# Second layer's value products: the high and the low part of the gated values side by side in one product of 448 columns

## The chip, the cores and the metric

One core of a Trainium2 chip. The metric is the device time of one execution in microseconds (us). The core's engines, by the names of the profile: PE (TensorE, products), PEld (its weight loads), DVE (VectorE), ACT (ScalarE), POOL (GpSimd) and SP (SyncE, which here issues most loads). Products write to accumulators in PSUM, whose banks hold 512 columns of 4 bytes for each of 128 partitions.

## The reference, cut to what matters

The model has two layers of mixers and a feed-forward part with 128 x 128 experts, of which each token takes 16 in each of 8 heads. The part around the change:

```python
eidx = jnp.take_along_axis(cand_i, fpos, axis=-1)
gate = jax.nn.softmax(fs, axis=-1)
act = jax.nn.gelu(jnp.einsum('td,thkd->thk', xb, u[eidx]).astype(F32), approximate=False)
w = (gate * act).astype(xb.dtype)
return jnp.einsum('thk,thkd->td', w, v[eidx])
```

The result f is added to the stream as x + g2 * f. Layer 0 has 512 tokens (256 of context, 256 latent), layer 1 only the 256 latent ones. At the end stands one more norm.

## The kernel before, in words

The kernel computes this densely for most tokens: every expert's activation for every token (u_blocks), times a gate that is zero for experts not chosen, times every expert's value row (v_blocks). 128 tokens of layer 0 and 32 of layer 1 are done apart by gathering their rows (tokens_apart, lines 1379 to 1435); so the dense products have wd = 384 columns in layer 0 and 224 in layer 1 (line 122).

Products at full precision are made of three products of a faster format. A number is split into a high part (a cast on ScalarE) and a low part (a subtraction on VectorE), and mm3 (lines 70 to 74) adds high x high, high x low and low x high:

```python
mm(ps, ah, bh, start=first, stop=False, **kw)
mm(ps, ah, bl, start=False, stop=False, **kw)
mm(ps, al, bh, start=False, stop=last, **kw)
```

The value stage of a layer (peer, lines 1179 to 1200) goes over 64 pairs of blocks; a block is 128 experts. For each pair, v_blocks

- loads 1 MB of values (line 1488) into one of two raw buffers;
- takes the pair's activations: for 20 of the pairs of layer 1 they have stayed in the tile "kept", already gated; otherwise they are loaded (va, line 1496), and the gates too, once for two pairs (vg, line 1493), and multiplied on VectorE (line 1500);
- splits the gated values into wh (ScalarE, line 1501) and wl (VectorE, line 1502), one instruction for both blocks, in a pool with two buffers in layer 0 and three in layer 1 (VA, line 33);
- splits each block's values into vh (line 1505) and vl (line 1506), in a pool of 10 buffers; a raw buffer is loaded again once both are done;
- issues the products: for each block and each of 8 output blocks d of 128 features, the three products of mm3 with vh or vl as weights and wh or wl as the moving operand, into the accumulator f of that d, columns 32 to 256 in layer 1. Each accumulator is one PSUM bank.

The loads go through SP's queue in the order in which they are issued. The engines' orders are made by the framework's planner from an estimate of durations, but for the last pair: there the order of TensorE, VectorE and ScalarE is that of the code (line 1530 on). In it the first block's products lead by three, each d gets its last products, the rows that were gathered for the tokens apart are added (line 1537), and then VectorE adds the accumulator, times g2, to the stream xt (line 1543). ScalarE squares xt (ss_add, line 338), VectorE adds squares in twos (line 340), and TensorE sums them over the partitions (line 346). In layer 1 the final norm and the output follow (final, lines 1554 to 1568).

Of the kernel before, what the change touches and what calls it, by code (L numbers as in the profile page):

```python
# [9 lines left out]
F32R = mybir.dt.float32r  # L10
# [4 lines left out]
ALU = mybir.AluOpType  # L15
# [38 lines left out]
class Kernel:  # L54
# [1425 lines left out]

    def v_blocks(self, l, n, i, acc, ts, off):

        w = self.wd[l]
        q = slice(off, off + w)
        parts = []
        nc, vp = self.nc, self.vp
        v = self.raw.tile([128, 2048], F32, name="raw").rearrange("p (b d) -> p b d", b=2)
        nc.sync.dma_start(v, self.A["v"][l, i:i + 2].rearrange("b p d -> p b d"))
        fold = i < 2 * FOLD[l]
        a = self.kept[:, i:i + 2] if fold else vp.tile([128, 2, w], F32, name="va")  # L1490
        if i % 4 == 0 and not fold:
            self.vg = vp.tile([128, w // 32, 4, 32], F32, name="vg", bufs=2)
            nc.sync.dma_start(self.vg[:, :w // 32].rearrange("p q b t -> p q (b t)"),
                              self.gd[l][:, :, i:i + 4].rearrange("q p b t -> p q (b t)"))
        if not fold:
            nc.sync.dma_start(a[:, :, :w], self.ad[l][i:i + 2].rearrange("b p t -> p b t"))
        wh, wl = (vp.tile([128, 2, w], F32R, name=x) for x in ("wh", "wl"))
        if not fold:
            av = a[:, :, :w].rearrange("p b (q t) -> p b q t", t=32)
            nc.vector.tensor_mul(av, av, self.vg[:, :w // 32, i % 4:i % 4 + 2].rearrange("p q b t -> p b q t"))  # L1500
        nc.scalar.copy(wh, a[:, :, :w])  # L1501
        nc.vector.tensor_tensor(wl, a[:, :, :w], wh.bitcast(F32), op=ALU.subtract)  # L1502
        for b in range(2):
            vh, vl = (self.spl.tile([128, 1024], F32R, name="spl") for _ in range(2))
            nc.scalar.copy(vh, v[:, b])  # L1505
            nc.vector.tensor_tensor(vl, v[:, b], vh.bitcast(F32), op=ALU.subtract)  # L1506
            parts.append((vh, vl, wh[:, b], wl[:, b]))

        def mm(d, b):
            c = slice(d * 128, (d + 1) * 128)  # L1510
            vh, vl, wh, wl = parts[b]
            self.mm3(acc[d][:, q], vh[:, c], vl[:, c], wh, wl, n + b == 0, n + b == 64)
        if n < 63:
            for b in range(2):
                for d in range(KD):
                    mm(d, b)
            return
        if l == 0:
            self.wraw, self.wspl = self.raw, self.spl
            self.nextg = self.gsplit(self.gload(self.A["win"][1, 9]))  # L1520
            self.nextq = self.wdma(self.A["win"][1, 2])
        full = ts.stop - ts.start
        if l == 0:
            big = [vp.tile([128, 2, 1024], F32, name="csb", bufs=1).rearrange("p a b -> p (a b)")]
            big += [vp.tile([128, 1024], F32, name="adaw", bufs=1), self.row_tile()]
            sqs = [t[:, a:a + 512] for t in big for a in range(0, t.shape[-1], 512)]
        else:
            sqs = [vp.tile([128, full], F32, name="sq", bufs=KD) for _ in range(KD)]
        self.ss_begin(sqs)
        with self.order("PE", "DVE", "Activation"):  # L1530
            lead = 3
            for d in range(lead):
                mm(d, 0)
            for d in range(KD):
                mm(d, 1)
                if off:
                    nc.tensor.matmul(acc[d][:, 0:off], self.facc[:, d * 128:(d + 1) * 128], self.fsel, start=True, stop=True)  # L1537
                if d + lead < KD:
                    mm(d + lead, 0)
                for s, seg in ((1, CTX), (0, LAT)):  # L1540
                    if seg.start >= ts.start:
                        o = slice(seg.start - ts.start, seg.stop - ts.start)
                        nc.vector.scalar_tensor_tensor(self.xt[:, d, seg], acc[d][:, o], self.mod[l][:, 5, d, s:s + 1],  # L1543
                                                       self.xt[:, d, seg], op0=ALU.mult, op1=ALU.add)
                if d == 1:
                    ps = self.pf.tile([128, 512], F32, name="f0")
                self.ss_add(d, self.xt[:, d, ts])
                if d > 2 and d % 2:
                    self.ss_mm((d - 3) // 2, ps)
            self.ss_mm(3, ps)  # L1550
            self.ss_mm(4, ps)
            self.ss_end(ps, full, 1024, self.ms, sqs[1])
# [250 lines left out]
```

## Time and profile before

| what | us |
|---|---|
| median of 3 runs (2806.03, 2815.85, 3308.41) | 2815.85 |
| the profiled execution | 2815.21 |
| its span | 2813.4 |
| second layer's value products, from about | 2431 |
| to about | 2800 |

In the rows, L73 is line 73 of the kernel; "f<-wl,spl" says that the instruction writes the tile f and reads wl and spl (vh and vl are both called spl, the raw values raw). Shapes are partitions x elements. "x1024" is a number of instructions. A duration in the profile is that of one instruction from its start to its modelled end; products overlap, so their pace is read from the distance of their starts, or from their number in a stretch without gaps. Arrows in a view of waits name who was waited for.

### The profile page before, as it was taken

The page shows a single profiled execution, that of the slowest core. Times are in us where ns is not written, and L with a number is a line of the kernel's source. Part 1 is how long each engine was busy: PE and PEld are TensorE (multiplying, and loading weights), DVE is VectorE, ACT ScalarE, POOL GpSimd, SP SyncE. Part 2 cuts the span into 40 slices and gives each one's busy share as a digit, 9 for nine tenths or more (in the row PEclk, how much of TensorE's full clock was granted, in tenths as well). Part 3 has the DMA queues.
Part 4 walks back from the last instruction along what each step waited for, and adds up shares of the span by engine and source line. Part 5 has one row for each costly group of instructions (what it writes and reads, how often), then busy time and mean ns, then how long its engine had stood idle before and what let it go on. Part 6 is the DMA issues. An engine that isn't in the chain of part 4 may idle for free. (4 is left out here: it accounts for less than half of the span.)

```text
span 2813.4 us, 46689 instructions
## 1 busy us (share of the span) xinstructions
PE 2649.8 (94%) x18167; PEld 2446.7 (87%) x18167; DVE 2166.6 (77%) x4491; ACT 1244.3 (44%) x2059; POOL 478.8 (17%) x419
## 2 busy tenths in 40 slices
PE   8989899999999998899999998988999999899998
PEld 5766768999998898899999997767899999899998
DVE  5665657999998875799999887555888778577765
ACT  5564635334443443333333334644544445344443
POOL 0010000003333333234333310100001101211110
PEclk9999899999999999899999999999999999999999
DMA  7110424647999989899999993202545878888884
GB/s 266 65 61 31 165 90 161 225 148 262 351 371 332 339 325 377 306 361 382 384 374 376 376 322 115 77 33 72 203 145 188 299 266 306 319 310 304 292 292 161
DMA packets 275742, 691.62 MB, mean 246 GB/s; under 512 B 18016, under 2 KB 145376, under 8 KB 266048
## 3 DMA queue, kind: packets, MB, share of 16 engines
q1 hardware_dynamic: 196608, 448.12, 45.6%
q0 software_dynamic: 46080, 167.79, 15.8%
q10 hardware_dynamic: 32832, 72.72, 6.9%
q8 instruction: 142, 2.33, 0.3%
q14 instruction: 80, 0.66, 0.1%
HBM read 616.56 MB, written 71.57 MB: 245 GB/s over the span
## 5 line engine op out<-in xcount | busy, mean ns | idle before, releaser
L72 PE MATMUL pu<-h2h,spl 128*128 128x384 f32 (+1 forms) x2048 | 637.3, 311 | 40.7 <-ACT spl L1448 27.7
L73 PE MATMUL f<-wl,spl 128*128 128x384 f32 (+1 forms) x2048 | 623.9, 306 | 8.0 <-DVE wl L1502 8.0
L74 PE MATMUL pu<-h2h,spl 128*128 128x384 f32 (+1 forms) x2048 | 628.9, 308 | 2.6 <-DVE spl L1449 2.6
L73 PE MATMUL pu<-h2l,spl 128*128 128x384 f32 (+1 forms) x2048 | 629.5, 307 | 0.0
L74 PE MATMUL f<-wh,spl 128*128 128x384 f32 (+1 forms) x2048 | 609.7, 305 | 2.3 <-DVE spl L1506 2.3
L72 PE MATMUL f<-wh,spl 128*128 128x384 f32 (+1 forms) x2048 | 568.4, 307 | 8.8 <-ACT act L1466 4.6
L72 PEld LDWEIGHTS pu<-h2h,spl 128*128 128x128 f32 x2048 | 393.2, 192 | 49.6 <-ACT spl L1448 32.4
L73 PEld LDWEIGHTS f<-wl,spl 128*128 128x128 f32 x2048 | 391.5, 191 | 10.9 <-DVE wl L1502 10.4
L74 PEld LDWEIGHTS pu<-h2h,spl 128*128 128x128 f32 x2048 | 392.7, 192 | 4.4 <-DVE spl L1449 4.2
L72 PEld LDWEIGHTS f<-wh,spl 128*128 128x128 f32 x2048 | 386.0, 191 | 10.7 <-ACT act L1466 5.0
L73 PEld LDWEIGHTS pu<-h2l,spl 128*128 128x128 f32 x2048 | 393.3, 192 | 0.3
L1505 ACT CAST spl<-raw 128x1024 fp32r<-128x1024 f32 x256 | 264.9, 1050 | 289.5 <-DMA raw<-in_v 202.8
L74 PEld LDWEIGHTS f<-wh,spl 128*128 128x128 f32 x2048 | 385.8, 191 | 2.8 <-DVE spl L1506 2.8
L1506 DVE TENSOR_TENSOR spl<-raw,spl 128x1024 fp32r<-128x1024 f32 x256 | 308.4, 1219 | 93.4 <-ACT spl L1505 85.1
L1448 ACT CAST spl<-raw 128x1024 fp32r<-128x1024 f32 x256 | 265.7, 1048 | 240.3 <-DMA raw<-in_ut 94.8
L1449 DVE TENSOR_TENSOR spl<-raw,spl 128x1024 fp32r<-128x1024 f32 x256 | 310.3, 1218 | 47.9 <-ACT spl L1448 38.3
L1409 POOL DMA_INDIRECT spl<-in_un,ix x97 | 129.3, 1333 | 716.7 <-DVE fp L1263 241.6
L1466 ACT ACTIVATE act<-pu 128x384 f32<-128x384 f32 (+1 forms) x216 | 93.0, 435 | 303.8 <-PE pu L74 280.7
L427 DVE TENSOR_TENSOR spl<-raw,spl 128x512 fp32r<-128x512 f32 (+1 forms) x226 | 149.4, 699 | 65.4 <-ACT spl L423 56.3
L1409 POOL DMA_INDIRECT row<-in_vn,ix x87 | 125.4, 1441 | 374.6 <-DVE facc L1422 316.3
L1501 ACT CAST wh<-va 128x768 fp32r<-128x768 f32 (+1 forms) x108 | 78.3, 725 | 231.3 <-DVE va L1500 131.6
L72 PE MATMUL fp<-s,spl 128*128 128x512 f32 (+1 forms) x416 | 161.2, 387 | 2.1 <-DVE s L666 1.2
(319 smaller groups left out, 4459.0 us busy)
## 6 DMA issues: line engine op xcount, KB each, us to landing
raw<-in_ut SPq DMA_DIRECT2D x128, 1024.0 KB
raw<-in_v SPq DMA_DIRECT2D x128, 1024.0 KB
ad<-act ACTq DMA_DIRECT2D x64, 384.0 KB
gd<-gstage ACTq DMA_DIRECT2D x12, 2048.0 KB
vg<-gd SPq DMA_DIRECT2D x32, 768.0 KB
va<-ad SPq DMA_DIRECT2D x64, 384.0 KB
raw<-in_win SPq DMA_DIRECT2D x22, 1024.0 KB
raw<-in_wq SPq DMA_DIRECT2D x16, 1024.0 KB
```

What stands on the lines that cost most here:

```text
L72: mm(ps, ah, bh, start=first, stop=False, **kw)
L73: mm(ps, ah, bl, start=False, stop=False, **kw)
L74: mm(ps, al, bh, start=False, stop=last, **kw)
L427: return eng.tensor_tensor(p[1][o], w[:, o], p[0][o].bitcast(F32), op=ALU.subtract)
L1409: nc.gpsimd.indirect_dma_start(r, None, tabs[which], bass.IndirectOffsetOnAxis(ix[:, s:s + 1], 0))
L1448: self.pin(nc.scalar.copy(uh, self.u[:, n % 2]), n < 3)
L1449: self.pin(nc.vector.tensor_tensor(ul, self.u[:, n % 2], uh.bitcast(F32), op=ALU.subtract), n < 3)
L1466: nc.scalar.activation(a[:, b, :w], ps[:, :w], AF.Gelu)
L1501: nc.scalar.copy(wh, a[:, :, :w])
L1505: nc.scalar.copy(vh, v[:, b])
L1506: nc.vector.tensor_tensor(vl, v[:, b], vh.bitcast(F32), op=ALU.subtract)
```

## The change

In layer 1 (wide = l > 0) wh and wl lie side by side in one tile wt, and each vh is multiplied with both at once: 448 columns, into columns 32 to 480 of the accumulator. The first 224 of them hold high x high, and low x high is added there as before; the other 224 hold high x low. At the end VectorE adds both halves to xt, one after the other. In the last pair's second block low x high goes ahead of the wide product, which closes the accumulation. In layer 0 only the tile is another; its products are those of mm3.

```diff
-        wh, wl = (vp.tile([128, 2, w], F32R, name=x) for x in ("wh", "wl"))
+        wide = l > 0
+        wt = vp.tile([128, 2, 2, w], F32R, name="wt")
+        wh, wl = wt[:, :, 0], wt[:, :, 1]
...
-            parts.append((vh, vl, wh[:, b], wl[:, b]))
+            parts.append((vh, vl, wh[:, b], wl[:, b], wt[:, b].rearrange("p a t -> p (a t)")))
 
         def mm(d, b):
             c = slice(d * 128, (d + 1) * 128)
-            vh, vl, wh, wl = parts[b]
-            self.mm3(acc[d][:, q], vh[:, c], vl[:, c], wh, wl, n + b == 0, n + b == 64)
+            vh, vl, wh, wl, both = parts[b]
+            first, last = n + b == 0, n + b == 64
+            if wide:
+                if last:
+                    nc.tensor.matmul(acc[d][:, q], vl[:, c], wh, start=False, stop=False)
+                nc.tensor.matmul(acc[d][:, off:off + 2 * w], vh[:, c], both, start=first, stop=last)
+                if not last:
+                    nc.tensor.matmul(acc[d][:, q], vl[:, c], wh, start=False, stop=False)
+            else:
+                self.mm3(acc[d][:, q], vh[:, c], vl[:, c], wh, wl, first, last)
...
+                if wide:
+                    seg = slice(ts.start + off, ts.stop)
+                    nc.vector.scalar_tensor_tensor(self.xt[:, d, seg], acc[d][:, off + w:off + 2 * w], self.mod[l][:, 5, d, 0:1],
+                                                   self.xt[:, d, seg], op0=ALU.mult, op1=ALU.add)
```

## Rows read from the trace of the kernel before

**Rows 1.** The page: busy time, share of the span and instructions of each engine.
```profile
PE 2649.8 (94%) x18167; PEld 2446.7 (87%) x18167; DVE 2166.6 (77%) x4491; ACT 1244.3 (44%) x2059; POOL 478.8 (17%) x419
```

**Rows 2.** Busy PE, PEld, DVE, ACT, POOL by stretch; granted clock, DMA share, GB/s.
```profile
2420.00:2440.00 20.00, 15.36 (x107) 14.99 (x107) 8.29 (x10) 5.41 (x9) 3.71 (x3) 0.83 1.05 389
1500.00:1520.00 20.00, 20.00 (x117) 20.00 (x116) 18.55 (x23) 7.41 (x8) 9.11 (x6) 1.00 1.04 386
2460.00:2520.00 60.00, 60.00 (x540) 60.00 (x539) 42.36 (x50) 27.44 (x33) 7.75 (x7) 1.00 0.89 315
2460.00:2780.00 320.00, 309.31 (x2732) 306.17 (x2731) 227.72 (x260) 140.67 (x172) 33.48 (x32) 1.00 0.86 294
```

**Rows 3.** Groups by line and shape, 2430 to 2813: busy, mean ns, idle before.
```profile
L73 PE MATMUL f<-wl,spl 128*128 128x224 f32 x1024 | 280.8, 277 | 8.0 <-DVE wl L1502 8.0
L72 PE MATMUL f<-wh,spl 128*128 128x224 f32 x1024 | 280.0, 277 | 6.7 <-ACT act L1466 4.6 <-ACT spl L1505 2.1
...
L1506 DVE TENSOR_TENSOR spl<-raw,spl 128x1024 fp32r<-128x1024 f32 x126 | 152.0, 1220 | 46.9 <-ACT spl L1505 44.4 <-PE f L73 1.3 <-PE f L74 1.0
L1505 ACT CAST spl<-raw 128x1024 fp32r<-128x1024 f32 x126 | 130.0, 1048 | 173.6 <-DMA raw<-in_v 155.2 <-PE f L73 10.4 <-PE f L74 8.0
...
L1500 DVE TENSOR_TENSOR va<-va,vg 128x448 f32<-128x448 f32 x44 | 27.4, 625 | 54.0 <-DMA va<-ad 32.8 <-issue 18.5 <-DVE wl L1502 2.8
L1502 DVE TENSOR_TENSOR wl<-va,wh 128x448 fp32r<-128x448 f32 x44 | 27.2, 620 | 6.5 <-ACT wh L1501 6.5
...
L1543 DVE SCALAR_TENSOR_TENSOR xt<-f,mod,xt 128x256 f32<-128x256 f32 x8 | 3.8, 481 | 5.6 <-PE f L1537 5.6
```

**Rows 4.** Who waited for whom, 2430 to 2813: us in total, times, longest.
```profile
ACT spl L1505 <- DMA raw<-in_v: 155.2, 50, 6.9
...
ACT wh L1501 <- PE f L74: 26.1, 10, 4.8
...
PE f L73 <- DVE wl L1502: 8.0, 12, 1.2
```

**Rows 5.** ScalarE in order of time: start, us, instruction, and the wait before it.
```profile
2517.37 1.05 ACT L1505 CAST spl<-raw 128x1024 fp32r<-128x1024 f32 x1 [4.01 <-DMA raw<-in_v]
...
2571.49 2.00 ACT L1505 CAST spl<-raw 128x1024 fp32r<-128x1024 f32 x2 [3.55 <-DMA raw<-in_v]
...
2588.94 1.05 ACT L1505 CAST spl<-raw 128x1024 fp32r<-128x1024 f32 x1 [5.56 <-PE f L73]
...
2644.92 1.05 ACT L1505 CAST spl<-raw 128x1024 fp32r<-128x1024 f32 x1 [3.35 <-DMA raw<-in_v]
...
2655.65 1.05 ACT L1505 CAST spl<-raw 128x1024 fp32r<-128x1024 f32 x1 [0.19 <-PE f L74]
...
2663.63 1.05 ACT L1505 CAST spl<-raw 128x1024 fp32r<-128x1024 f32 x1 [5.51 <-DMA raw<-in_v]
...
2760.98 1.05 ACT L1505 CAST spl<-raw 128x1024 fp32r<-128x1024 f32 x1 [3.41 <-DMA raw<-in_v]
```

**Rows 6.** SyncE's queue in order of time: the issue of one value load.
```profile
2656.99 0.37 SPq L1488 DMA_DIRECT2D raw<-in_v  x1
```

**Rows 7.** TensorE in order of time: first and last of 13 products of 512 columns.
```profile
438.12 0.40 PE L73 MATMUL mm<-h2l,spl 128*128 128x512 f32 x1
...
440.86 0.39 PE L73 MATMUL mm<-h2l,spl 128*128 128x512 f32 x1
```

**Rows 8.** VectorE in order of time at the end of the value stage.
```profile
2793.99 0.48 DVE L1543 SCALAR_TENSOR_TENSOR xt<-f,mod,xt 128x256 f32<-128x256 f32 x1 [4.74 <-PE f L1537]
...
2796.20 0.96 DVE L1543 SCALAR_TENSOR_TENSOR xt<-f,mod,xt 128x256 f32<-128x256 f32 x2
2797.64 0.43 DVE L340 TENSOR_TENSOR sq<-sq 128x256 f32<-128x256 f32 x1 [0.48 <-ACT sq L338]
2798.00 0.48 DVE L1543 SCALAR_TENSOR_TENSOR xt<-f,mod,xt 128x256 f32<-128x256 f32 x1
...
2800.20 0.87 DVE L1543 SCALAR_TENSOR_TENSOR xt<-f,mod,xt 128x256 f32<-128x256 f32 x2
```

## The prediction

> **What bounds the kernel now.** I read the first lines of the page first: TensorE's products are busy 2649.8 of 2813.4 us [rows 1], so work taken off TensorE can count, if nothing else in that stage is just as slow. The share is an average over stages, so I then cut out the one stage that the change touches, the second layer's value products, from about 2431 to 2800 us. In the table of stretches [rows 2] the reader is to see three things: in 2460 to 2520 the products are busy without a gap and 540 of them start in 60 us; over the whole of 2460 to 2780 they are busy 309.3 of 320 us; and the transfers run at 0.86 to 0.89 of the DMA engines while this goes on. The groups by line [rows 3] give the counts: each of the three product lines (72 and 73 stand there) starts 1024 products of 224 columns in this stage, and the two splits of the values run 126 times each in that window. Their last part is the waiting time of the engine in front of the line: TensorE waits 8.0 + 2.1 us on operands and 4.6 us on the stage before, which is little. The view of who waited for whom gives the other half: ScalarE waits 155.2 us in 50 pieces for the 1 MB loads of values, against 26.1 us in 10 [rows 4] and 10.4 + 8.0 us [rows 3] for TensorE to give a buffer back.
>
> So two paces lie close together: that of the products, and that of the supply (load, cast, subtraction, next load into the same one of two buffers). I call two blocks that come with one load a pair; the stage has 64. The products of a pair are 48, at 60 us / 540 = 111 ns each: 5.33 us. The supply is read from the starts of each pair's first cast, in stretches that show ScalarE waiting for loads alone from behind their first cast on [rows 5]. From 2517.37 to 2571.49 lie 10 pairs, 5.41 us each; from 2588.94 to 2644.92 another 10, 5.60 each; from 2655.65 to 2760.98 lie 18, 5.85 each. There the supply is already the slower one, and TensorE gets through on the blocks it has in hand. In one of these stretches a load that is issued at 2656.99 [rows 6] is waited for until 2663.63 [rows 5], 6.6 us; a buffer then spends two casts of 1.05 us and two subtractions of 1.22 us [rows 3] before it is loaded again, and VectorE has the gate products and the gathered rows between them. Nothing in that ring is a product.
>
> **The products.** The change takes away 2 x 1024 products of 224 columns (lines 72 and 73) and adds 1024 of 448. No product of 448 columns stands in the trace, so its pace is bounded by neighbours at the full clock: 384 columns go at 20 us / 117 = 171 ns [rows 2], 512 columns at (440.86 - 438.12) / 12 = 228 ns [rows 7]. Half way between 384 and 512 lies 448: 200 ns, which I take. Two narrow products cost 222 ns, so one merge saves 22 ns, and the stage 1024 x 22.2 ns = 22.7 us of TensorE's time, or 0.355 us a pair; by the ends it would be 52 us saved or 6 us lost. The reason for a saving is in the same rows: 224 columns take 111 ns, and 384 take only 60 ns more for 160 columns, 0.375 ns a column, so some 27 ns of a product don't grow with its columns by these two, and one such part goes with each merge; by 384 and 512, whose slope is 0.445 ns, it is nearly nothing. That is why I go by the point between the two nearest and not by either line.
>
> One rule stands against a saving. The Trainium skill (TensorE: Matmul & The Clock Gate, section "Wait — 56ns, not 53.3ns?") says that back-to-back products start N / 2.4 GHz plus about 2.5 ns apart once the clock is up. The rows don't agree with it at 224 columns: 111 ns stand against 95.8 ns by the rule, and 228 against 215.8 at 512. By the rule a merge would save only its 2.5 ns, an estimate of 2.6 us for the stage, and with the longer end below the kernel would come out where it was.
>
> **What of it reaches the end.** In the 38 pairs of the three stretches the supply sets the pace, and faster products only wait longer: nothing gained. In the other 26 pairs TensorE has no gap or holds the buffers (the 26.1 + 10.4 + 8.0 = 44.5 us that ScalarE waits for it), and I count the full gain: 26 x 0.355 = 9.2 us. The lower end for this term is 0, if the supply takes over at once there too (with 4.98 us a pair it would need 5.33 / 4.98 x 315 = 337 GB/s in the stretch of [rows 2] that now moves 315; 389 and 386 GB/s stand in other rows there, so the transfers as such allow it). The upper end is all 22.7 us, if supply is slow only because TensorE gives buffers back late.
>
> **The end of the stage.** The value stage's end now has eight more operations on VectorE, each 128 x 224, which add the second half of the accumulator. The same operation on 256 columns takes 0.481 us [rows 3]; for 224 I take 0.45, bounds 0.42 and 0.48. They can't hide. Today the updates of the end run from 2793.99 to 2800.20 + 0.87 = 2801.07 [rows 8], with gaps in which VectorE waits for the products. In the middle, from 2796.20 to 2798.00, two blocks take VectorE 1.80 us: two updates of 0.48, then 0.48 of waiting for ScalarE's square, then an addition of 0.43. Two more updates make that 2.70. Three such rounds and a last one of 4 operations, 1.77, are 9.87 us against 7.08 now: +2.8 us, on the path; bounds 2.4 and 3.5. Each square now waits for the second update of its block, which is in the 2.70. Behind it the same norm, root and output follow. In the last block the order of the two products is turned round; their number is that of the others.
>
> **What I count at nothing.** The two halves of the gated values become one tile. Its buffers are as many (two in the first layer, three in the second), and the last reader of the pair is the same low-part product, so buffers come free when they did. The casts write two runs of 224 with a gap instead of 448 in one; the gate product, which reads the gates in such pieces, takes 0.625 us against 0.620 for the subtraction [rows 3], so a gap costs some 5 ns, 64 x 3 x 5 ns = 1 us of two engines with room. The wide product waits for the subtraction that makes the low half; today its second narrow product does, one product later: at most 0.11 us in each of 12 waits [rows 4], 1.3 us. Were VectorE's order such that this subtraction came after one more of 1.22 us in every pair, 64 x 1.22 = 78 us would be the end of it; the order is planned anew, and nothing shows it. In the first layer only the tile changes and no product; TensorE is busy 20.00 of 20 us there [rows 2].
>
> **Sum.** The profiled execution took 2815.2 us, 1.8 us of it around its span of 2813.4, and the median of the three runs is 2815.85, so the two are one number here. 2815.2 - 9.2 + 2.8 = 2808.8, say 2809 us.
>
> **Rivals.** First, products pace the whole stage: all 22.7 us arrive, 2815.2 - 22.7 + 2.8 = 2795. For it: TensorE is busy 309 of 320 us. Against it: the 155.2 us of waiting for loads, and intervals above 5.33 us in 38 pairs. Second, slower than before: the supply takes over in the other 26 pairs as well, from the point where a pair of supply takes 5.33 us, and the longer end is all that is left: 2815.2 + 2.8 = 2818, and 2825 if the wide product goes no better than 512 columns do (228 ns, 1024 x 6 ns). For it: the stretch from 2460 to 2520 already runs the transfers at 0.89. Against it: the 44.5 us in which ScalarE waits for TensorE show a supply that is ahead in those pairs. Beside it stands a drop of the granted clock when gaps grow: 2420 to 2440, where the stage before ends and TensorE was busy 15.36 of 20 us, had a mean of 0.83 and 107 products where 180 fit [rows 2]; such a thing all through would cost far more. Third, only the columns count and a merge is worth nothing: 448 columns at 2 x 111 ns, gain 0, and the end's 2.8, 2818 again, told from the second by the pace of the wide products; the line through 384 and 512 columns speaks for it, the one through 224 and 384 against it. By the Trainium skill's rule above, an estimate of 2.6 us would be gained here, and the sum be 2815.
>
> **How the numbers follow.** Forecast 0.5, centre 2809, by itself 2800 to 2814. Products pace everything: 0.2, around 2795. Supply paces everything: 0.17, 2818 to 2825. Only columns count: 0.08, 2818. An order of VectorE or of the loads that is planned worse: 0.05. Two of the three runs of before, 2806.03 and 2815.85, lie 10 us apart, so the range reaches to both first rivals and a little over: 2790 to 2823. Two per cent are 56 us, about what a measurement of this kernel can tell from no change. A gain over it would need the 384 columns' pace and a supply that follows: 0.01. A loss over it needs the bad order or the clock: 0.03. Within: 0.96.
>
> **What would show it.** Right, step by step: 1024 products of 128 x 448 and 1024 fewer products in all; wide products starting 200 ns, narrow ones 111 ns apart in a stretch without gaps; ScalarE's waits for the value loads longer than 155 us and its waits for TensorE shorter than 44.5; TensorE's own waits in the stage up from some 15 to some 28 us; 16 updates at the end and 2.8 us more from the first to the last. Wrong: wide products at 215 ns or more, a stage shorter by 20 us, waits of TensorE for the low half in most pairs, or a difference that lies in the first layer.

## The result, and the profile after

| | before | after |
|---|---|---|
| median of 6 runs each, us | 2813.07 | 2798.97 |
| the profiled execution, us | 2815.21 | 2801.05 |
| its span, us | 2813.4 | 2799.3 |

The ratio is 0.9942, with an interval of 0.9917 to 0.9967: some 16 us less (9 to 23). It leaves out before's run of 3308.41 us, which was in a slower state. The forecast was 6.4 us less. That lies below the interval; the stated range, 2790 to 2823 us, holds the result.

Where the 14.1 us between the two spans lie can be added up from starts in TensorE's and VectorE's order of time. I cut at the last activation product (writes pu), the first value product (writes f), the first update of xt and the end of the last update:

| stretch, us | before | after | difference |
|---|---|---|---|
| start to last activation product | 2427.54 | 2427.28 | -0.3 |
| to the first value product ("gap") | 4.3 | 1.7 | -2.6 |
| to the first update ("stage") | 362.1 | 347.6 | -14.5 |
| to the end of the last update | 7.1 | 9.9 | +2.8 |
| to the end of the span | 12.3 | 12.9 | +0.5 |

The 2.6 us of the gap are hardly the change's: three other kernels with the wide products (4, 9 and 10 below) have gaps of 3.6 to 3.9 us.

The first line of the page of after stands against [rows 1]: 1024 products fewer, 21.5 us less of them.

```profile
PE 2628.3 (94%) x17143; PEld 2407.9 (86%) x17143; DVE 2168.7 (77%) x4499; ACT 1249.8 (45%) x2059; POOL 490.9 (18%) x419
```

TensorE of after in order of time (start, us, instruction), in a stretch without gaps, gives the new pace:

```profile
2486.11 1.79 PE L1519 MATMUL f<-wt,spl 128*128 128x448 f32 x8
2487.74 1.05 PE L1521 MATMUL f<-wt,spl 128*128 128x224 f32 x8
2488.63 1.79 PE L1519 MATMUL f<-wt,spl 128*128 128x448 f32 x8
2490.26 1.05 PE L1521 MATMUL f<-wt,spl 128*128 128x224 f32 x8
2491.14 1.79 PE L1519 MATMUL f<-wt,spl 128*128 128x448 f32 x8
```

Eight wide products take 2487.74 - 2486.11 = 1.63 us, 204 ns each; eight narrow ones 0.89 us, 111 ns each. A pair, 16 of each, takes 2491.14 - 2486.11 = 5.03 us (forecast 4.98). Before, in a stretch without gaps, the first products of the sixth and of the fifteenth pair are these:

```profile
2466.25 0.28 PE L72 MATMUL f<-wh,spl 128*128 128x224 f32 x1
...
2514.49 0.28 PE L72 MATMUL f<-wh,spl 128*128 128x224 f32 x1
```

That is 48.24 / 9 = 5.36 us a pair; the 5.33 of the prediction came from a count in a window. The products of a stage alone are then 64 x 5.03 = 322 us, against 64 x 5.36 = 343 us before. I call what a stage takes above that lost: 19 us before, 26 after. So some 21 us were saved and 7 of them given back. (The stage ends with the first update, when some 3.5 us of products are still to come; every row is too low by that.) Not all that is lost is waiting. TensorE's waits add up to 12.9 us before and 19.7 after; in the stage's first 24 us the granted clock is below 1.00 as well, before and then after (columns as in [rows 2]):

```profile
2432.00:2456.00 24.00, 21.76 (x149) 21.39 (x150) 16.82 (x22) 7.29 (x11) 2.02 (x2) 0.79 0.95 326
```
```profile
2429.00:2453.00 24.00, 18.48 (x93) 16.64 (x94) 14.29 (x19) 7.08 (x10) 1.08 (x1) 0.86 0.89 303
```

Stretches of after, columns as in [rows 2]:

```profile
2460.00:2520.00 60.00, 58.83 (x373) 55.46 (x371) 45.07 (x54) 29.32 (x35) 8.22 (x8) 1.00 0.92 322
...
2450.00:2760.00 310.00, 295.87 (x1850) 276.98 (x1849) 232.50 (x267) 145.24 (x176) 37.34 (x33) 1.00 0.88 309
```

In 2460 to 2520, where TensorE had no gap before, it now has 1.2 us of them, and the transfers went from 315 to 322 GB/s.

Groups by line of after, 2430 to 2800 (columns as in [rows 3]):

```profile
L1519 PE MATMUL f<-wt,spl 128*128 128x448 f32 x1023 | 250.6, 372 | 15.6 <-ACT spl L1508 11.7 <-DVE wt L1505 3.3 <-ACT act L1466 0.6
...
L1521 PE MATMUL f<-wt,spl 128*128 128x224 f32 x1015 | 156.0, 274 | 4.0 <-DVE spl L1509 3.9
...
L1505 DVE TENSOR_TENSOR wt<-va,wt 128x448 fp32r<-128x448 f32 x44 | 27.2, 621 | 9.0 <-ACT wt L1504 9.0
L1504 ACT CAST wt<-va 128x448 fp32r<-128x448 f32 x44 | 24.9, 566 | 44.0 <-PE f L1521 30.1 <-DVE va L1503 7.3 <-issue 6.5
```

TensorE now waits for the cast of a block's values (11.7 us), and before for the low half of the gated values (8.0 us, [rows 3]). The splits of the gated values cost what they did: 621 ns on VectorE. Who waited for whom in after, same stretch, against [rows 4]:

```profile
ACT spl L1508 <- DMA raw<-in_v: 131.1, 57, 5.1
...
ACT wt L1504 <- PE f L1521: 37.9, 29, 7.6
```

ScalarE waits *less* for the value loads than before (131 us against 155), though the products are faster. That doesn't fit a supply that is as it was, and it led to the order of the instructions. Before, second half of the stage, ScalarE and then VectorE in order of time:

```profile
2652.99 1.05 ACT L1505 CAST spl<-raw 128x1024 fp32r<-128x1024 f32 x1 [5.59 <-PE f L74]
2653.94 0.56 ACT L1501 CAST wh<-va 128x448 fp32r<-128x448 f32 x1
2654.41 1.05 ACT L1505 CAST spl<-raw 128x1024 fp32r<-128x1024 f32 x1
```
```profile
2654.07 1.23 DVE L1506 TENSOR_TENSOR spl<-raw,spl 128x1024 fp32r<-128x1024 f32 x1 [2.54 <-ACT spl L1505]
2655.21 0.62 DVE L1502 TENSOR_TENSOR wl<-va,wh 128x448 fp32r<-128x448 f32 x1
2655.74 1.22 DVE L1506 TENSOR_TENSOR spl<-raw,spl 128x1024 fp32r<-128x1024 f32 x1
```

After, the same two engines:

```profile
2706.40 2.00 ACT L1508 CAST spl<-raw 128x1024 fp32r<-128x1024 f32 x2 [4.29 <-DMA raw<-in_v]
2708.31 0.56 ACT L1504 CAST wt<-va 128x448 fp32r<-128x448 f32 x1
```
```profile
2707.48 2.36 DVE L1509 TENSOR_TENSOR spl<-raw,spl 128x1024 fp32r<-128x1024 f32 x2 [3.69 <-ACT spl L1508]
2709.76 1.28 DVE L1422 SCALAR_TENSOR_TENSOR facc<-row,wt,facc 128x1024 f32<-128x1024 f32 x1
2710.95 0.62 DVE L1505 TENSOR_TENSOR wt<-va,wt 128x448 fp32r<-128x448 f32 x1
```

Before, the gated values are split *between* the two blocks of values; after, both blocks go through in one piece ("x2") and the gated values of the next pair come behind them, that is *ahead* of their own pair's blocks. Counted on VectorE over the 64 pairs: before, from the 27th pair on, the gated split stands after the first block's subtraction in 37 of 38 pairs; after, it stands ahead of both in 37 of them. From the first cast to the end of the second subtraction a raw buffer is held 5.2 us on average in pairs 27 to 63 before, and 4.0 us after; in the first 26 pairs, where the order of before is "ahead" too almost throughout, 4.2 and 4.2. Only then can it be loaded again. With two buffers in turn, 1.2 us of holding are 0.6 us a pair, and the first casts did come closer: over these pairs 5.20 us each after (2577.24 to 2764.27) and 5.70 before (2575.74 to 2780.88).

### The profile page after: what moved, and what is told of

Its sections match the earlier page's. It is cut to its first block, busy times and chain, and to the rows that moved or that the text cites. A ratio compares the mean times of both kernels' runs of the same rounds, so it can differ in the third digit from the quotient of the medians.

```text
span 2799.3 us, 44568 instructions
## 1 busy us (share of the span) xinstructions
PE 2628.3 (94%) x17143; PEld 2407.9 (86%) x17143; DVE 2168.7 (77%) x4499; ACT 1249.8 (45%) x2059; POOL 490.9 (18%) x419
## 5 line engine op out<-in xcount | busy, mean ns | idle before, releaser
L1508 ACT CAST spl<-raw 128x1024 fp32r<-128x1024 f32 x256 | 261.9, 1051 | 256.5 <-DMA raw<-in_v 173.6
L73 PE MATMUL f<-wt,spl 128*128 128x384 f32 x1024 | 343.2, 335 | 0.0
L74 PE MATMUL f<-wt,spl 128*128 128x384 f32 x1024 | 336.3, 334 | 0.0
L72 PE MATMUL f<-wt,spl 128*128 128x384 f32 x1024 | 288.4, 337 | 2.1 <-ACT spl L1508 1.9
L1519 PE MATMUL f<-wt,spl 128*128 128x448 f32 x1024 | 251.1, 372 | 17.1 <-ACT spl L1508 11.7
L1519 PEld LDWEIGHTS f<-wt,spl 128*128 128x128 f32 x1024 | 186.0, 190 | 33.3 <-ACT spl L1508 15.0
L73 PEld LDWEIGHTS f<-wt,spl 128*128 128x128 f32 x1024 | 193.0, 188 | 0.5 <-issue 0.5
L74 PEld LDWEIGHTS f<-wt,spl 128*128 128x128 f32 x1024 | 191.6, 188 | 0.0
L72 PEld LDWEIGHTS f<-wt,spl 128*128 128x128 f32 x1024 | 187.9, 189 | 3.2 <-ACT spl L1508 2.2
```

Source lines behind the costliest of these rows:

```text
L1519: nc.tensor.matmul(acc[d][:, off:off + 2 * w], vh[:, c], both, start=first, stop=last)
```

## The experiments

My theory before them: the products save what was forecast, and the planner's other order lets more of it through. Rivals: the new tile does it; the loads themselves are the limit; the buffers of the gated values are. All ratios are against the kernel before, run on the same chip beside them. The medians come from several chips, on which the kernel before had 2809 (kernels 1 to 4), 2818 (5 to 8) and 2813 us (9 to 11), so they don't compare across these groups; the ratios do. "Lost" is the stage less the products' own 343 or 322 us.

| kernel | median, us | ratio, 95% interval | gap | stage | lost |
|---|---|---|---|---|---|
| before (its profile) | | 1 | 4.3 | 362.1 | 19 |
| after (its profile) | 2798.97 | 0.9942, 0.9917 to 0.9967 | 1.7 | 347.6 | 26 |
| 1 tile only | 2811.32 | 0.9999, 0.9986 to 1.0013 | 4.1 | 368.6 | 26 |
| 2 before, ahead | 2803.70 | 0.9976, 0.9961 to 0.9991 | 0.1 | 362.8 | 20 |
| 3 after, between | 2806.03 | 0.9977, 0.9963 to 0.9992 | 2.5 | 356.4 | 34 |
| 4 after, no second update | 2795.44 | 0.9937, 0.9914 to 0.9959 | 3.9 | 345.3 | 23 |
| 5 before, no loads | 2808.75 | 0.9978, 0.9960 to 0.9997 | 1.4 | 359.6 | 17 |
| 6 after, no loads | 2801.42 | 0.9938, 0.9915 to 0.9961 | 1.5 | 339.5 | 18 |
| 7 before, third raw buffer | 2801.98 | 0.9948, 0.9929 to 0.9967 | 10.2 | 342.8 | 0 |
| 8 after, third raw buffer | 2781.26 | 0.9878, 0.9851 to 0.9904 | 10.2 | 321.1 | -1 |
| 9 after, three rows | 2797.77 | 0.9945, 0.9928 to 0.9962 | 3.7 | 345.9 | 24 |
| 10 after, four gated buffers | 2801.94 | 0.9959, 0.9941 to 0.9978 | 3.6 | 347.3 | 25 |
| 11 after, no loads, ahead | 2775.03 | 0.9866, 0.9845 to 0.9887 | 0.1 | 326.8 | 5 |

Gap and stage are of one profile each. Before and kernel 1 issue the same products in the same kind of order and lie 6.5 us apart in the stage, so for kernels of that kind smaller differences in these columns say nothing; after, 4, 9 and 10 agree within 2.3 us. What stands ahead of the stage varies more: the last activation product starts between 2417 and 2437 us in these profiles, though VectorE, ScalarE and GpSimd have the same order in all of them up to 30 us before it.

The order changed only from the 27th pair on, so it helps to cut the stage there. A pair's 48 or 32 products are counted off in TensorE's order of time, which gives the start of the 27th pair's first product:

| kernel | first 26 pairs, us | 27th pair to the first update, us |
|---|---|---|
| before | 149.0 | 213.2 |
| 1 tile only | 155.1 | 213.5 |
| 2 before, ahead | 157.1 | 205.6 |
| 3 after, between | 148.3 | 208.0 |
| after | 151.0 | 196.6 |
| 4, 9 and 10 | 146.6, 146.7, 143.5 | 198.7, 199.2, 203.8 |

Before and kernel 1 lie 6.1 us apart in the first part and 0.3 in the second, where the order is at stake.

**1. Tile only.** The side-by-side tile stays, the products are the three narrow ones.

```diff
-        wide = l > 0
+        wide = False
```


> One tile for both halves in both layers, but three narrow products in the second layer as before; no second half, so no second updates. Theory P (the planner, given shorter products, puts the split of the gated values ahead of both value splits; that order feeds the products faster and brought some 5 us) and theory F (the shorter products alone give buffers back earlier; the order brought nothing) both expect what the kernel before shows: 362 us from the first value product of the second layer to the first update of the stream, 2813 us in all, within 3 us. A third theory, T (the one tile itself brought part of the gain), expects 3 to 5 us less than before.

0.9999: the tile does nothing to the time. The stage of its one profile, 368.6 us, lies outside the 362 within 3 that was expected; all but 0.3 us of the difference to before lies in the first 26 pairs. VectorE's order here is that of before, the gated split between the blocks. The change of order thus comes with the wide product. That it comes through the planner's estimate of durations is how the planner works; no run shows it by itself.

**2. The order alone.** The kernel before, with the first block's cast and subtraction held in program order, that is behind the pair's gated split. This holds them against the sums over gathered rows too, which were held already.

```diff
+            early = l > 0 and b == 0 and n < 63
-            nc.scalar.copy(vh, v[:, b])
-            nc.vector.tensor_tensor(vl, v[:, b], vh.bitcast(F32), op=ALU.subtract)
+            self.pin(nc.scalar.copy(vh, v[:, b]), early)
+            self.pin(nc.vector.tensor_tensor(vl, v[:, b], vh.bitcast(F32), op=ALU.subtract), early)
```


> The kernel before, with the splits of a pair's values held behind the split of its gated values in the second layer, so that VectorE goes gated, value, value instead of value, gated, value; products unchanged. Theory P expects 5 us less than before: 357 instead of 362 us from the first value product to the first update, 2808 us in all, and less waiting of TensorE for the low half (8.0 us now). Theory F expects no difference beyond 2 us.

0.9976, 6.7 us less with not one product changed. The stage of its profile is no shorter than before's, against the 357 us that theory P expected. Cut at the 27th pair, it is 7.6 us shorter (213.2 to 205.6) where the order was changed, and 8.1 longer in the first 26 pairs, where the gated split stood ahead before, too; there the same kernel can differ by as much as before and kernel 1 do. So the order is worth some 7 us to the narrow products. TensorE's waits for the low half fell from 8.0 to 2.0 us.

**3. The wide product alone.** After, with the gated values' split held between the two blocks.

```diff
+        between = l > 0 and n < 63
+        if not between:
-        nc.scalar.copy(wh, a[:, :, :w])
-        nc.vector.tensor_tensor(wl, a[:, :, :w], wh.bitcast(F32), op=ALU.subtract)
+            nc.scalar.copy(wh, a[:, :, :w])
+            nc.vector.tensor_tensor(wl, a[:, :, :w], wh.bitcast(F32), op=ALU.subtract)
...
+            after = between and b == 1
-            nc.scalar.copy(vh, v[:, b])
-            nc.vector.tensor_tensor(vl, v[:, b], vh.bitcast(F32), op=ALU.subtract)
+            self.pin(nc.scalar.copy(vh, v[:, b]), after)
+            self.pin(nc.vector.tensor_tensor(vl, v[:, b], vh.bitcast(F32), op=ALU.subtract), after)
+            if between and b == 0:
+                self.pin(nc.scalar.copy(wh, a[:, :, :w]))
+                self.pin(nc.vector.tensor_tensor(wl, a[:, :, :w], wh.bitcast(F32), op=ALU.subtract))
```


> The kernel after, with the split of the gated values held between the splits of the pair's two value blocks (value, gated, value), the order that the kernel before had in its second half; wide products unchanged. Theory P expects 5 to 10 us more than after: 353 to 358 instead of 347.6 us from the first value product to the first update, 2804 to 2809 us in all. Theory F expects 347.6 within 2 us, 2799 us in all.

0.9977, 6.5 us less (2 to 10), and the stage within what theory P expected. Who waited for whom in it, 2430 to 2790:

```profile
ACT spl L1511 <- DMA raw<-in_v: 173.6, 56, 5.7
...
PE f L1525 <- DVE wt L1515: 27.6, 21, 4.6
```

ScalarE waits more for loads than the 155.2 us of [rows 4], and TensorE 27.6 us for the low half. 34 us are lost, and the stage gains only 5.7 on before's. After, which differs in the order alone, has a stage 8.8 us shorter; a raw buffer is held 4.6 us here and 4.0 there, which with two buffers is 0.3 us a pair, some 11 us over pairs 27 to 63; from the 27th pair on the two lie 208.0 - 196.6 = 11.4 us apart. From there on kernel 3 has the order of before, and only the products differ: 213.2 to 208.0, 5.2 us. A raw buffer is held 4.6 us instead of 5.2, so in this part the shorter products do reach the ring. Order alone, products alone and both make 7.6, 5.2 and 16.6 us there (9.4 to 14.5 in kernels 4, 9 and 10).

**4. Without the second updates.** The eight additions of the accumulator's second half are left out, and so is high x low from the result.

```diff
-                if wide:
-                    seg = slice(ts.start + off, ts.stop)
-                    nc.vector.scalar_tensor_tensor(self.xt[:, d, seg], acc[d][:, off + w:off + 2 * w], self.mod[l][:, 5, d, 0:1],
-                                                   self.xt[:, d, seg], op0=ALU.mult, op1=ALU.add)
```


> The kernel after without the eight updates that add the second half of the accumulator; the high by low part of the second layer's value products is left out of the output. Every theory expects 2.8 us less from the first to the last update (7.1 instead of 9.9 us), and 3 us less in all: 2796 us. If the end hides the eight updates after all, nothing changes.

First and last row of its updates on VectorE:

```profile
2774.05 0.48 DVE L1554 SCALAR_TENSOR_TENSOR xt<-f,mod,xt 128x256 f32<-128x256 f32 x1 [3.67 <-PE f L1548]
...
2780.04 0.87 DVE L1554 SCALAR_TENSOR_TENSOR xt<-f,mod,xt 128x256 f32<-128x256 f32 x2
```

2780.91 - 2774.05 = 6.9 us against 9.9 with them: 3.0 us by the profile. The timing can't separate it: 0.9937 and 0.9942 lie inside each other's intervals.

**5 and 6. Without the loads.** Only the first two pairs' values are loaded in layer 1; the other 62 loads are left out, and those pairs use the old values. Before (5) and after (6).

```diff
+        if l == 0 or n < 2:
             v = self.raw.tile([128, 2048], F32, name="raw").rearrange("p (b d) -> p b d", b=2)
             nc.sync.dma_start(v, self.A["v"][l, i:i + 2].rearrange("b p d -> p b d"))
+            self.vkeep = [v] if n % 2 == 0 else self.vkeep + [v]
+        else:
+            v = self.vkeep[n % 2]
```


> The kernel before, with the second layer's values loaded for the first two pairs only; the other 62 pairs split and multiply these again, so the layer's output isn't the reference's. With no value load to wait for, every theory expects the products' own pace, 64 pairs at 5.36 us: 348 us (343 and a start of some 5) instead of 366.5 from the last activation product of the second layer to the first update of the stream, 2797 us in all. If it stays above 360, something other than the loads (VectorE, the gates, the gathered rows) held the products.

> The kernel after, with the same 62 value loads left out. Theory S (the supply of values still holds the wide products back in part of the pairs; a merge saves 20.8 ns, 21 us in the stage) expects 64 pairs at 5.03 us: 327 us instead of 349.3 from the last activation product to the first update, 2778 us in all, and 18 us less than the kernel before without these loads (21 us of products, 2.8 back at the end). Theory C (the change has brought all that its products have to give) expects 345 or more, 14 us less than the kernel before without loads at the most.

Both miss: 17 and 18 us stay lost, where the theory of a supply limited by its loads wanted next to nothing. The planner had changed the order once more. In both kernels the gated split now stands between the blocks, or behind both, and TensorE waits for it, while VectorE waits for the gated values' own loads. Who waited for whom in kernel 6, 2430 to 2790:

```profile
DVE va L1507 <- DMA va<-ad: 55.9, 32, 4.3
...
PE f L1523 <- DVE wt L1509: 16.0, 9, 6.3
```

So taking the loads away says nothing while the order is free; kernel 11 holds it.

**7, 8 and 9. A third raw buffer.** Before (7) and after (8) get a third buffer for the values of layer 1, paid for with one of the four of the gathered rows. Kernel 9 is the control: after, with three buffers of rows and still two raw ones.

```diff
+                    if l:
+                        self.raw3 = ep2(tc.tile_pool(name="raw3", bufs=1, reuse_waits="tile"))
-                        rows = ep2(tc.tile_pool(name=f"rows{l}", bufs=ROWS, reuse_waits="tile"))
+                        rows = ep2(tc.tile_pool(name=f"rows{l}", bufs=ROWS - l, reuse_waits="tile"))
...
-        v = self.raw.tile([128, 2048], F32, name="raw").rearrange("p (b d) -> p b d", b=2)
+        pool = self.raw3 if l and n % 3 == 2 else self.raw
+        v = pool.tile([128, 2048], F32, name="raw").rearrange("p (b d) -> p b d", b=2)
```


> The kernel before, with a third raw buffer for the second layer's value loads (every third pair uses it) and three buffers instead of four for that layer's gathered rows, to make room. Theory S (the ring of load, two casts, two subtractions in two buffers sets the pace where TensorE waits) expects most of the 18 us between 366.5 and 348 back: 352 to 356 us from the last activation product to the first update, 2800 us in all. A rival, B (the transfers as such are as fast as they go, at 0.86 of the DMA engines), expects no difference beyond 3 us.

> The kernel after, with the same third raw buffer and three buffers for gathered rows. Theory S expects TensorE's waits for value splits (13.9 us from 2450 to 2770) below 5 us, 332 to 340 us instead of 349.3 from the last activation product to the first update, and 2785 to 2790 us in all, the fastest version so far. B expects 349 and 2799: at 5.03 us a pair the stage would move 318 GB/s where it moves 306.

> The kernel after with three buffers instead of four for the second layer's gathered rows and still two raw buffers: the price of the room that the third raw buffer took. Theory S (the third raw buffer alone brought the 18 us between after and after with three) expects nothing: 349 us from the last activation product to the first update, 2799 us in all. The rival, that fewer rows under way at a time (less in the transfers' way) brought it, expects 331 and 2781.

All three go the way theory S expected: 353.0, 331.3 and 349.6 us from the last activation product, kernel 8 a little better than its 332 to 340. With a third buffer TensorE hardly waits in either stage (0.7 and 0.0 us), and the stages differ by 342.8 - 321.1 = 21.7 us: what the merges save, undisguised. The stretch 2450 to 2760 of kernel 8 (columns as in [rows 2]), and its waits from 2430 to 2790:

```profile
2450.00:2760.00 310.00, 310.00 (x1976) 295.44 (x1974) 248.09 (x283) 153.19 (x188) 39.32 (x34) 1.00 0.92 321
```
```profile
ACT wt L1507 <- PE f L1524: 139.0, 55, 4.1
...
ACT spl L1511 <- DMA raw<-in_v: 10.7, 1, 10.7
```

TensorE is busy in all of the 310 us (after: 295.87 of them), and the loads come at 321 GB/s. The 131 us in which ScalarE waited for loads are gone but for one wait at the stage's start, and in their place it waits for TensorE. The transfers as such were not the limit, the turn-round of two buffers was. Fewer rows alone change nothing (0.9945). Kernel 8, at 0.9878, is faster than both kernels of this case, 34 us below before. It still has a gap of 10.2 us at the start, in which that one wait stands.

**10. Four buffers for the gated values** instead of three, with three of rows.

```diff
-FOLD, QS, VA = (0, 20), (10, 6), (2, 3)
+FOLD, QS, VA = (0, 20), (10, 6), (2, 4)
```


> The kernel after with four instead of three buffers for the activations and the gated values (room from the gathered rows, three instead of four), and two raw buffers. Theory S (the raw ring sets the pace) expects nothing beyond 3 us: 346 to 350 us from the last activation product to the first update. The rival G (ScalarE's 37.9 us of waiting for a buffer of gated values hold up the casts of the values behind it) expects 335 to 340, 2788 us in all.

0.9959 and a stage of 347.3 us, that of after. With the gap that is 350.9 us, 0.9 above what was expected and far from the rival's 335 to 340: these buffers are not the limit.

**11. Without the loads, order held.** Kernel 6 (62 loads left out) with the edit of kernel 2.

> The kernel after with 62 of the second layer's 64 value loads left out as before, and the split of the gated values held ahead of both value splits of a pair; the layer's output isn't the reference's. If it was VectorE's order (value, gated, value, planned anew without the loads) that kept the wide products waiting 16 us for the low half without the loads, those waits go and 327 to 335 us lie between the last activation product and the first update, 2782 us in all. If the loads of activations and gates hold it, whatever the order, it stays at 341.

The stage is 326.8 us, 5 us lost, and no wait of TensorE stands between 2450 and the stage's end. Between kernels 6 and 11 only the order differs: 12.7 us of the stage and 0.9938 against 0.9866. So the miss of kernel 6 was the order's. For kernel 5 that is likely by its waits, but no run holds its order.

## Why the prediction was right or wrong

**The products: right.** 204 ns for 448 columns against 200 forecast, 111 for 224, so a merge saves 18 ns by these starts and 21 by the pace of a pair (5.36 less 5.03 us over 16 merges), where I had 22. The 21.7 us of kernels 7 and 8 stand against 22.7. The midpoint between 384 and 512 columns was the right row to go by. The rule of the Trainium skill (TensorE: Matmul & The Clock Gate, "Wait — 56ns, not 53.3ns?"), by which a merge would save its 2.5 ns, doesn't describe these products: 204 ns stand against an estimate of 189 by the rule, and kernels 7 and 8 show some eight times its saving.

**What of it reaches the end: wrong by place, near by luck.** I counted 9.2 of 22.7 us, less 2.8 at the end: 6.4. Kernel 3, with the order of before's second half throughout, gives 6.5, but not where I had put it. My 38 pairs, counted at nothing, take 218.4 us before and 213.5 in kernel 3; the other 26, counted at 9.2, take 143.7 and 142.8. In after they take 209.1 and 138.5, so 9.3 us came where I had nothing and 5.2 where I had 9.2. (Kernel 1, with before's products and order, has 222.3 and 146.3, so a few us of this are spread.) Two steps failed. In the 26 pairs the supply took over in part as soon as the products were faster: TensorE, without gaps from 2460 to 2520 before, has them after. The lower end of my term had this. In the 38 pairs "faster products only wait longer" was too strong, for with the order of before kernel 3 still gains there. That the supply, through its two buffers, holds TensorE back is shown by kernels 7 and 8, where a third buffer ends nearly all waits.

**Wrong: the step "What I count at nothing".** It said of the bad order of VectorE that "the order is planned anew, and nothing shows it", and set an order that is better at nothing without naming it. The planner works from durations, the change alters them, and the order did change: the gated split left the ring of load, cast, subtraction and release. I had written that nothing in that ring is a product, and had read the rows of its casts; that a third instruction, the gated split, stood *in* the ring in one half of the stage and not in the other was there to be seen. Between kernel 3 and after this is 0.9977 against 0.9942, some 10 us, of which the profiles show 8.8 in the stage and 0.8 in the gap. That is as much as the result lies below the forecast, though the intervals of the two ratios, 2 to 10 and 9 to 23 us, leave room.

**The waits.** "ScalarE's waits for loads longer than 155 us" was wrong (131.1) and right with the order held (173.6). "Its waits for TensorE shorter than 44.5" was right by the one row that is left, 37.9. TensorE's own, forecast at 28 us from 15, are 15.6 + 4.0 = 20 in after, and 27.6 in kernel 3 for the low half alone.

**The end: right to a tenth.** Sixteen updates, of which the first starts at 2776.59 and the last ends at 2786.45: 9.86 us against 9.87 forecast and 7.08 in [rows 8]. One round of them on VectorE:

```profile
2779.27 0.48 DVE L1554 SCALAR_TENSOR_TENSOR xt<-f,mod,xt 128x256 f32<-128x256 f32 x1
2779.78 0.45 DVE L1558 SCALAR_TENSOR_TENSOR xt<-f,mod,xt 128x224 f32<-128x224 f32 x1
2780.15 0.48 DVE L1554 SCALAR_TENSOR_TENSOR xt<-f,mod,xt 128x256 f32<-128x256 f32 x1
2780.66 0.45 DVE L1558 SCALAR_TENSOR_TENSOR xt<-f,mod,xt 128x224 f32<-128x224 f32 x1
2781.59 0.43 DVE L340 TENSOR_TENSOR sq<-sq 128x256 f32<-128x256 f32 x1 [0.48 <-ACT sq L338]
```

The next round starts at 2781.94, 2.67 us after this one (forecast 2.70). What I missed there is half a microsecond behind it, told below.

**The rivals.** Products pacing everything (2795) lies 4 us from what came, but by another way than its own: supply didn't follow TensorE, it was replanned, and TensorE still lost 26 us. Only kernels 7 and 8 have a stage that the products pace. Supply pacing everything (2818) falls by the time itself, and columns alone by the pace of the wide products and by kernel 7 against 8. What stays open is how much of the 9 to 17 us from the 27th pair on is the order's and how much the products', as one profile of each kernel tells them apart only to a few us, and whether the second updates could be taken off the end, which wasn't tried.

## What to carry to other kernels

Where a planner sets the order from estimated durations, a change of one duration can also be a change of order: look in the trace for a ring (load, cast, subtraction, release), ask which instructions stand in it only by the planner's choice, and give a better order a price as well as a worse one. Two products with the same weights side by side in one saved 18 to 21 ns each here, but it arrives only as far as buffers let the supply follow; a third load buffer was worth as much again as the change. An experiment that removes work under such a planner needs its order held, or it measures the new order. And a total that agrees proves little: cut the stage where the mechanism should act, and see whether the gain lies there.

## What the runs showed of the hardware that I had not expected

The clock at the very end. Before, TensorE ran without a gap into its last six sums of squares, which took 1.97 us; after, the second updates make it wait first, 0.60 us and then 0.97, and the same six take 3.43:

```profile
2782.07 0.70 PE L346 MATMUL f<-sq,ones 128*128 128x256 f32 x2 [0.60 <-DVE sq L340]
...
2784.74 3.43 PE L346 MATMUL f<-sq,ones 128*128 128x256 f32 x6 [0.97 <-DVE sq L340]
```

Busy time by stretch of after, on either side of that wait (columns as in [rows 2]):

```profile
2776.00:2784.00 8.00, 7.16 (x47) 6.42 (x46) 6.01 (x14) 2.28 (x6) 0.00 (x0) 1.00 0.00 1
2784.00:2789.00 5.00, 3.32 (x6) 1.50 (x6) 2.62 (x9) 1.06 (x3) 0.13 (x1) 0.66 0.00 0
```

The granted clock is 1.00 and then 0.66 on average, where 1 stands for 2.4 GHz and the lower level is 1.2; before it was 1.00 from 2800 to 2803. In kernel 4, without the second updates and their waits, the six take 1.97 us again. But the waits don't bring the lower clock each time. In kernel 8 the same two stand, and the six go in pairs at a granted clock of 1.00 (2772 to 2777):

```profile
2770.21 0.70 PE L346 MATMUL f<-sq,ones 128*128 128x256 f32 x2 [0.60 <-DVE sq L340]
...
2772.88 0.70 PE L346 MATMUL f<-sq,ones 128*128 128x256 f32 x2 [0.98 <-DVE sq L340]
2774.21 0.70 PE L346 MATMUL f<-sq,ones 128*128 128x256 f32 x2 [0.63 <-ACT sq L338]
2775.09 0.70 PE L346 MATMUL f<-sq,ones 128*128 128x256 f32 x2 [0.18 <-ACT sq L338]
```

They end 2.9 us after their start, waits for the squares included, against 3.43 in after, and from the last update to the end of the span it is 12.3 us, as before. So the lower clock costs the 0.5 us in the last line of the first table: little, and seen here only behind waits that additions on another engine brought.
